# Laying out the probabilities one step later in paged decode attention: a hybrid decoder step on one core

## The chip, the cores and the metric

The kernel runs on one NeuronCore of a Trainium2 chip. The metric is the device time of one execution in microseconds, median of several. The kernel before takes 1250.35 us (three runs, 1250.27 to 1250.57). The profile is of one further execution.

## What is computed

One layer of a hybrid decoder, for a prompt of 512 tokens and for 8 sample sequences of 4 new tokens each, with shared float32 weights: a gated FFN, a mixer (four heads of a gated linear recurrence and four heads of latent attention), and a second gated FFN. The part that matters here is the attention of the sample tokens over 4096 cached rows per sequence, which are fetched through a page table:

```python
past_c = cache_kv_latent[l][page_table].reshape(Bs, past_len, KV_LORA)
past_r = cache_k_rope[l][page_table].reshape(Bs, past_len, QK_ROPE)
...
s = (jnp.einsum('bqhr,bsr->bhqs', ql, c_kv) + jnp.einsum('bqhd,bsd->bhqs', qr, k_rope)).astype(jnp.float32) * scale
s = jnp.where(k_pos[None, None, None, :] <= qp[None, None, :, None], s, -jnp.inf)
p = jax.nn.softmax(s, axis=-1).astype(c_kv.dtype)
return jnp.einsum('bhqs,bsr->bqhr', p, c_kv)
```

## The kernel before

Most of the time is weight matrices. A weight tile (`wraw`, 128x8x128 float32) is loaded by SyncE's DMA queue, split by ScalarE into a rounded high part `wh` (L250) and by VectorE into the rest `wl` (L251), and multiplied with activations that are split in the same way, three matmuls for each product (L259, L277, L288).

The second FFN runs twice: once for the first 256 prompt tokens and once for the others. **Decode runs beside the first of these passes.** `decode()` and the FFN `gb` are two Python generators that the program advances in turn (100 FFN steps over 94 steps of decode). The sample attention is cut into 16 **halves**, two for each sequence: half n is sequence n//2, 2048 cached rows in two gathered blocks. They are called half 0 to half 15 below. Every half goes through a pipeline of five steps `st` = 0 to 4 for each value of n:

- `gather` and `gather_r` (L1366, L1373): GpSimd issues the indirect DMAs for the latent rows (`craw`, seven places: `ulb uhb ha hb mb q0 dx`) and rotary rows (`rraw`, two places).
- `turn(st)` (L1381): VectorE transposes the keys in blocks of 32x32, two instructions for each of five turns, into `kh` (four buffers). Turn 0 takes the rotary rows, turns 1 to 4 take latent columns.
- `score` (L1393): TensorE multiplies. Turns 0 to 2 are used at step 2 (96 row-column groups of matmuls), turns 3 and 4 at step 4 (64). The last of them ends the score, and ScalarE and VectorE copy it to SBUF (L1399); VectorE takes its row maximum (L1401).
- `peak` (L1405 to L1417), at step 1 of the next n: TensorE spreads the maximum (`pm`), VectorE reduces it and makes the bias, ScalarE takes the exponential in place (L1411), VectorE transposes the probabilities into `pt` (L1413), and sixteen small copies place `pt` into `pbuf`, the stationary operand of the value product: four on VectorE, twelve on ScalarE (L1417). `pbuf` and `pt` have two buffers each.
- `value` (L1426), at step 4: TensorE multiplies `pbuf` with the gathered rows, 32 matmuls, 16 for each block. Each run of four matmuls waits for the `pbuf` copies of its own quarter, so for three more of ScalarE's twelve.

In one n, `at(2)` is the half whose scores are computed and `at(3)` the half in front of it, whose peak and value are computed. So at step 4 TensorE has, in this order and with nothing between them, the matmuls of turns 3 and 4 of half k+1 and the value matmuls of half k. Turn 3 is made at step 1 and turn 4 at step 2.

The order of instructions on each engine is not that of the Python code alone: a list scheduler with priorities may move an instruction past others on the same engine. The engines then take their instructions strictly in the order of the compiled program.

The lines touched are those of `peak` (it ends after L1411 and its rest becomes a new function) and the loop of `decode` (`if st == PEAK and at(3)`, with PEAK = 1).

Of the kernel before, what the change touches and what calls it, by code (L numbers as in the profile page):

```python
# [66 lines left out]
PEAK = 1  # L67
# [43 lines left out]
def hybrid_step_kernel(  # L111
# [18 lines left out]
    def mk(shape, dt, tag, bufs=1, pool=None):  # L130
        return (pool or cur[-1]).tile(shape, dt, name=tag, tag=tag, bufs=bufs)
# [10 lines left out]
    def ps(name, tag="ps", own=False):  # L142
        if tag == "ps" and not own:
            tag = CYC[turns[0] % 4]
            turns[0] += 1
        return pp.tile([P, 512], F32, name=name, tag=tag, bufs=NPS[tag])
# [422 lines left out]
    with scope("ffn0") as pool:  # L569
# [143 lines left out]
        if True:  # L713
            if True:
                sst.close()
                st = stg.enter_context(tc.tile_pool(name="st", bufs=1, side="right", reuse_waits="tile"))
# [585 lines left out]
    with scope("dec"):  # L1302
# [49 lines left out]
        class Half:  # L1352
# [50 lines left out]
            def peak(self):  # L1403
                pm = ps("pm", "pm")[:, :P]
                nc.tensor.matmul(pm, self.mx.broadcast_to([P, P]), ident, start=True, stop=True, skip_group_check=True)  # L1405
                m = m3[:, self.i, self.bs]
                nc.vector.tensor_reduce(m, pm.rearrange("p (g q) -> p q g", q=16), axis=AX.X, op=ALU.max)
                mq = mk([P, 16], F32, "mq", 2)
                mb = mk([P, 1], F32, "mbd", 2)
                nc.vector.scalar_tensor_tensor(mq, m, -SCALE, selL, op0=ALU.mult, op1=ALU.mult, accum_out=mb)  # L1410
                nc.scalar.activation(self.e, self.e, AF.Exp, scale=SCALE, bias=mb, accum_out=Lc[:, self.i, 0, self.b : self.b + 1])  # L1411
                pt = mk([P, ROWS, 32], F32, "pt", 2)
                nc.vector.transpose(pt.rearrange("p a k -> p (a k)"), self.e)  # L1413
                for c in range(4):
                    for g in range(4):
                        src = pt[c * 32 : c * 32 + 32, g // 2 * 4 : g // 2 * 4 + 4, g % 2 * 16 : g % 2 * 16 + 16]
                        (nc.scalar.copy if g else nc.vector.tensor_copy)(self.p[g * 32 : g * 32 + 32, c // 2, c % 2 * 4 : c % 2 * 4 + 4, self.i * 16 : self.i * 16 + 16], src)  # L1417
# [19 lines left out]
        def decode():  # L1437
            H = [Half(n) for n in range(NH2)]
            blocks = [h_ for h_ in H for _ in range(2)]
            ups = [(h_, st) for h_ in H for st in range(len(JS))]  # L1440

            def gather(n=1):
                for h_ in blocks[:n]:
                    h_.gather()
                del blocks[:n]

            def turn(top):
                if ups:
                    h_, st = ups.pop(0)
                    with tc.issue_after(top.ins) if top is not None else nullcontext():  # L1450
                        h_.turn(st)
                    if st == 0 and h_.n + 1 < NH2:
                        H[h_.n + 1].gather_r()

            for n in range(NH2 + 4):

                def at(k):
                    return H[n - k] if 0 <= n - k < NH2 else None

                for st in range(len(JS)):  # L1460
                    if at(2):
                        for k in RUNS.get(st, ()):
                            at(2).score(k)
                    if n < 3 and st == 0:
                        if n == 0:
                            H[0].gather_r()
                        gather(2 + n // 2)
                    if st == PEAK and at(3):
                        at(3).peak()
                    if st == 1 and at(4) and at(4).i:  # L1470
                        at(4).gathered()
                    if st == len(JS) - 1 and at(3):
                        for c in range(2):
                            at(3).value(at(4), c)
                            gather()
                    if n > 1 or n == 1 and st >= 1:
                        if n != 2 or st >= 2:
                            turn(at(2).top if at(2) and st == len(JS) - 1 else None)
                    yield

        def decode_end():
# [33 lines left out]
            nc.vector.tensor_copy(oT[1][:, NH:, HS[1] - TS :], o[:, :P].rearrange("p (h t) -> p h t", h=NH))  # L1515

        ga, gn = decode(), decode_new()
        na, ib = len(JS) * (NH2 + 2) + 4, 0
        for ia in range(na):
# [190 lines left out]
```

## Time and profile before

| | |
|---|---|
| median of the runs | 1250.35 us |
| profiled execution, whole | 1243.16 us |
| its span in the trace | 1241.4 us |
| mean granted TensorE clock | 0.999 |
| decode beside the FFN, in the trace | about 711 to 955 us |
| the 16 `pt` transposes (L1413), one for each half | start at 734.9 to 946.9 us, 436 ns each in the median |

The profile's times are those of one execution. "Busy" of an engine is the time in which one of its instructions runs; TensorE's weight loads (PEld) have a row of their own and run ahead of its matmuls. A bracket such as `[0.85 <-DVE pt L1413]` behind an instruction says how long its engine had been idle before it, and what ended that wait. Rows with a count (x12) merge like instructions that follow each other. In the traces the buffers of the pools are called by short names: `q` stands for several small tiles.

### The profile page before, as it was taken

The numbers are of one execution on the slowest core, as the hardware profiler recorded it, in microseconds if no ns is written. First come the engines' busy times: TensorE is split into PE (matmuls) and PEld (weight loads), VectorE is DVE, ScalarE is ACT, GpSimd is POOL, SyncE is SP. The second block draws the span as 40 slices with busy tenths as digits, with TensorE's granted clock in tenths as the row PEclk, the third lists the DMA queues.
The fourth block names the chain that finished last, engine by engine and source line by source line (L and its number), as shares of the span: only waits on it lengthen the run. The fifth ranks groups of instructions, "written<-read, shape, count | busy, mean of one in ns | idle before, by whom it ended". The sixth has DMA issues, their size and how long they took to land.

```text
span 1241.4 us, 29997 instructions
## 1 busy us (share of the span) xinstructions
PE 1215.0 (98%) x12366; PEld 1151.3 (93%) x12366; DVE 982.7 (79%) x1976; ACT 738.8 (60%) x1559; POOL 76.5 (6%) x80
## 2 busy tenths in 40 slices
PE   8999999999999999999999999999999999999997
PEld 6999999999999989988898888888888999999997
DVE  7897788878678888786877899999998778566665
ACT  7675545455366744545758766666656776554455
POOL 0000000000000000000001312322310000000000
PEclk9999999999999999999999999999999999999999
DMA  6232333232264213333233868878776635545451
GB/s 238 86 115 90 103 103 102 86 99 91 62 221 147 82 54 105 88 94 130 85 105 117 339 214 303 310 282 323 258 275 232 198 106 188 184 137 188 150 151 60
DMA packets 73113, 195.59 MB, mean 158 GB/s; under 512 B 12336, under 2 KB 27728, under 8 KB 68240
## 3 DMA queue, kind: packets, MB, share of 16 engines
q1 hardware_dynamic: 64512, 150.47, 37.3%
q0 software_dynamic: 7168, 41.95, 9.2%
q8 instruction: 97, 1.59, 0.5%
q10 hardware_dynamic: 1296, 1.26, 0.3%
q14 instruction: 40, 0.33, 0.1%
HBM read 183.97 MB, written 9.67 MB: 156 GB/s over the span
## 4 chain that ended last, share of the span: by engine, by line
PE 79%; DVE 11%; ACT 7%; issue 2%; DMA 2%; SPq 0%; DVEq 0%; ACTq 0%
PE acc L259 29%; PE acc L277 13%; PE dn L259 8%; PE Y L575 7%; PE X L575 4%; PE Z L575 4%; DVE kh L1381 3%; PE acc L731 3%; DVE wl L251 2%; ACT wh L250 1%; PE s L1393 1%; ACT pbuf L1417 1%; DMA wraw<-w_g 1%; PE pa L952 1%; PE o L1426 1%
## 5 line engine op out<-in xcount | busy, mean ns | idle before, releaser
L250 ACT CAST wh<-wraw 128x1024 fp32r<-128x1024 f32 (+2 forms) x194 | 185.0, 957 | 164.3 <-PE acc L259 103.7
L251 DVE TENSOR_TENSOR wl<-wraw,wh 128x1024 fp32r<-128x1024 f32 (+2 forms) x194 | 214.6, 1108 | 72.2 <-ACT wh L250 71.6
L277 PE MATMUL acc<-uha,wh 128*128 128x256 f32 (+1 forms) x528 | 155.5, 295 | 0.1
L277 PE MATMUL acc<-uha,wl 128*128 128x256 f32 (+1 forms) x528 | 150.0, 285 | 0.8 <-DVE wl L251 0.7
L277 PE MATMUL acc<-ula,wh 128*128 128x256 f32 (+1 forms) x528 | 150.5, 286 | 0.0
L259 PE MATMUL acc<-uhb,wh 128*128 128x288 f32 (+1 forms) x432 | 128.0, 296 | 0.0
L259 PE MATMUL acc<-uhb,wl 128*128 128x288 f32 (+1 forms) x432 | 127.0, 295 | 1.0 <-DVE wl L251 0.8
L259 PE MATMUL acc<-ulb,wh 128*128 128x288 f32 (+1 forms) x432 | 127.5, 295 | 0.0
L277 PEld LDWEIGHTS acc<-uha,wh 128*128 128x128 f32 x528 | 99.2, 188 | 8.8 <-issue 7.9
L277 PEld LDWEIGHTS acc<-uha,wl 128*128 128x128 f32 x528 | 99.2, 188 | 2.3 <-DVE wl L251 1.6
L277 PEld LDWEIGHTS acc<-ula,wh 128*128 128x128 f32 x528 | 99.4, 188 | 1.6 <-issue 1.2
L259 PEld LDWEIGHTS acc<-uhb,wl 128*128 128x128 f32 x432 | 81.2, 188 | 1.6 <-DVE wl L251 1.6
L259 PEld LDWEIGHTS acc<-uhb,wh 128*128 128x128 f32 x432 | 81.0, 187 | 0.2 <-ACT uhb L170 0.2
L259 PEld LDWEIGHTS acc<-ulb,wh 128*128 128x128 f32 x432 | 81.1, 188 | 0.1
L259 PE MATMUL dn<-hh,dh 128*128 128x272 f32 x256 | 74.3, 290 | 0.0
L259 PE MATMUL dn<-hh,dl 128*128 128x272 f32 x256 | 73.7, 288 | 0.0
L259 PE MATMUL dn<-hl,dh 128*128 128x272 f32 x256 | 73.6, 288 | 0.0
L277 PE MATMUL acc<-uhb,wh 128*128 128x272 f32 x176 | 52.8, 300 | 0.0
L1417 ACT COPY pbuf<-pt 32x64 f32<-32x64 f32 x192 | 46.5, 242 | 10.1 <-DVE pt L1413 7.3
L259 PE MATMUL acc<-hlb,wh 128*128 128x288 f32 x176 | 52.1, 298 | 0.0
L259 PE MATMUL acc<-hhb,wh 128*128 128x288 f32 x176 | 51.8, 298 | 0.0
L1393 PE MATMUL s<-kh,q 64*32 64x128 f32 x2560 | 48.0, 273 | 3.5 <-DVE kh L1381 3.5
(632 smaller groups left out, 3881.3 us busy)
## 6 DMA issues: line engine op xcount, KB each, us to landing
wraw<-w_u SPq DMA_DIRECT2D x66, 512.0 KB, 4.3
wraw<-w_g SPq DMA_DIRECT2D x65, 512.0 KB, 3.9
wraw<-w_d SPq DMA_DIRECT2D x40, 384.0 KB, 3.5
wraw<-w_in SPq DMA_DIRECT2D x24, 512.0 KB, 3.5
wraw<-w_d SPq DMA_DIRECT2D x32, 320.0 KB, 3.1
wraw<-w_d SPq DMA_DIRECT2D x16, 512.0 KB, 3.8
wraw<-w_o SPq DMA_DIRECT2D x16, 512.0 KB, 3.7
g_S<-state SPq DMA_DIRECT2D x4, 512.0 KB, 4.4
```

The lines of the kernel that those rows point to most:

```text
L250: nc.scalar.copy(wh[:, :kt], w[:, :kt])
L251: nc.vector.tensor_tensor(wl[:, :kt], w[:, :kt], f32(wh[:, :kt]), op=ALU.subtract)
L259: nc.tensor.matmul(out, a, b, start=n == 0, stop=n == last)
L277: nc.tensor.matmul(acc[:, :n], a[:, k], b[:, k], start=k + i == 0, stop=k == kt - 1 and i == 2)
L575: nc.tensor.matmul(bank, a[p][:, k], b[q][:, k], start=first and k + n == 0, stop=k == 3 and n == 2, skip_group_check=True)
L731: nc.tensor.matmul(accs[x, d], wts[d][p][:, k], hs[k // 2][q][:, k % 2, x], start=k + n == 0, stop=k == nf - 1 and n == 2)
L952: nc.tensor.matmul(po[es, c].rearrange("p (n m) -> p n m", m=m), kx[:, cs], up(qx[:, cs], m), start=True, stop=True, skip_group_check=True)
L1381: nc.vector.transpose(kh[:, g].rearrange("p a j k -> p a (j k)"), src)
L1393: nc.tensor.matmul(self.s[r][c * 32 : c * 32 + 32, :P], q[rs, j], kh, start=st + jj == 0, stop=st == len(JS) - 1 and jj == 1, skip_group_c ...
L1417: (nc.scalar.copy if g else nc.vector.tensor_copy)(self.p[g * 32 : g * 32 + 32, c // 2, c % 2 * 4 : c % 2 * 4 + 4, self.i * 16 : self.i * ...
L1426: nc.tensor.matmul(o[g : g + 32, :R], self.p[:, c, a], self.craw[c][:, a], start=i + c == 0 and a < 4, stop=i + c == 2 and a >= 4, skip_gr ...
```

## The change

`peak` stops after the exponential. Its rest, the transposition of the probabilities and the sixteen copies, becomes `lay`, which is called at the end of step 2 (PEAK + 1), behind that step's turn, which is turn 4.

```diff
                 nc.scalar.activation(self.e, self.e, AF.Exp, scale=SCALE, bias=mb, accum_out=Lc[:, self.i, 0, self.b : self.b + 1])
+
+            def lay(self):
                 pt = mk([P, ROWS, 32], F32, "pt", 2)
                 nc.vector.transpose(pt.rearrange("p a k -> p (a k)"), self.e)
...
                         if n != 2 or st >= 2:
                             turn(at(2).top if at(2) and st == len(JS) - 1 else None)
+                    if st == PEAK + 1 and at(3):
+                        at(3).lay()
                     yield
```

No instruction is added or taken away. TensorE's order is the same row for row, and so are those of SyncE's and GpSimd's queues. ScalarE's order differs in three halves: in half 0 two parts of a sigmoid come between the twelve copies, and in halves 2 and 3 one copy of an FFN result (L390) comes ahead of them instead of behind. VectorE's order is the same in halves 2, 3, 9, 12 and 15 and differs in the others. Three places follow.

VectorE in half 4 (`hb` and `mb` are the two blocks of half 5, so `kh<-hb` and `kh<-mb` are turn 4; `kh<-rraw` is turn 0 of half 6). Before:

```order
L251 TENSOR_TENSOR wl<-wraw,wh 128x1024
L1413 STREAM_TRANSPOSE pt<-q_8192 128x256
L171 TENSOR_TENSOR hla<-sil,hha 128x256
L1417 COPY pbuf<-pt 32x4x16 x4
L1381 STREAM_TRANSPOSE kh<-hb 128x512
L1381 STREAM_TRANSPOSE kh<-mb 128x512
L1381 STREAM_TRANSPOSE kh<-rraw 128x512 x2
L334 TENSOR_TENSOR sil<-acc,rna 128x256
```

And now:

```order
L251 TENSOR_TENSOR wl<-wraw,wh 128x1024
L171 TENSOR_TENSOR hla<-sil,hha 128x256
L1381 STREAM_TRANSPOSE kh<-hb 128x512
L1381 STREAM_TRANSPOSE kh<-mb 128x512
L1415 STREAM_TRANSPOSE pt<-q_8192 128x256
L1381 STREAM_TRANSPOSE kh<-rraw 128x512
L1419 COPY pbuf<-pt 32x4x16 x4
L1381 STREAM_TRANSPOSE kh<-rraw 128x512
L334 TENSOR_TENSOR sil<-acc,rna 128x256
```

Both transposes of turn 4 and one FFN row have moved ahead of `pt`, and one rotary transpose ahead of the copies. Halves 1, 7 and 10 change in the same way, and half 13 does but for one transpose of turn 4 that stood ahead of `pt` already. In halves 0, 5 and 11 `pt` keeps its place in front of turn 4, and only copies move behind the second transpose of it; in half 8 one copy moves behind both.

VectorE in half 6 (`ulb` and `uhb` are the blocks of half 7). Before:

```order
L1413 STREAM_TRANSPOSE pt<-q_8192 128x256
L1381 STREAM_TRANSPOSE kh<-ulb 128x512
L1417 COPY pbuf<-pt 32x4x16 x4
L1381 STREAM_TRANSPOSE kh<-uhb 128x512
L336 TENSOR_TENSOR sil<-sil,sit 128x256
```

And now:

```order
L1381 STREAM_TRANSPOSE kh<-ulb 128x512
L1381 STREAM_TRANSPOSE kh<-uhb 128x512
L1415 STREAM_TRANSPOSE pt<-q_8192 128x256
L336 TENSOR_TENSOR sil<-sil,sit 128x256
L1419 COPY pbuf<-pt 32x4x16 x4
```

Here `pt` moves behind two transposes, and the copies behind an FFN row as well.

VectorE in half 14 (`ha` and `hb` are the blocks of half 15). Before:

```order
L1413 STREAM_TRANSPOSE pt<-q_8192 128x256
L392 TENSOR_TENSOR ma<-ma,acc 128x256
L1417 COPY pbuf<-pt 32x4x16 x4
L1381 STREAM_TRANSPOSE kh<-ha 128x512
L1381 STREAM_TRANSPOSE kh<-hb 128x512
L251 TENSOR_TENSOR wl<-wraw,wh 128x1024
```

And now:

```order
L392 TENSOR_TENSOR ma<-ma,acc 128x256
L1415 STREAM_TRANSPOSE pt<-q_8192 128x256
L251 TENSOR_TENSOR wl<-wraw,wh 128x1024
L1381 STREAM_TRANSPOSE kh<-ha 128x512
L1381 STREAM_TRANSPOSE kh<-hb 128x512
L1419 COPY pbuf<-pt 32x4x16 x4
```

Here a weight split that stood behind turn 4 has moved ahead of it.

## The prediction

> **What bounds the kernel now.** I read the page first, then the busy time by stretches, the waits, and the instructions around single halves.
>
> ```profile
> span 1241.4 us, 29997 instructions
> PE 1215.0 (98%) x12366; PEld 1151.3 (93%) x12366; DVE 982.7 (79%) x1976; ACT 738.8 (60%) x1559; POOL 76.5 (6%) x80
> ```
>
> TensorE is busy for 98% of the span, so a change that leaves its work alone can win only its gaps. The change moves instructions of decode only, so the stretches of decode count. Their columns are start and end, length, then busy us of PE, PEld, DVE, ACT and POOL, the clock, and the DMA share:
>
> ```profile
> 755.00:797.00 42.00, 42.00 (x747) 37.97 (x740) 38.02 (x80) 26.46 (x70) 12.42 (x12) 1.00 0.92 329
> 797.00:840.00 43.00, 41.44 (x855) 35.34 (x858) 40.87 (x93) 28.31 (x82) 12.87 (x13) 1.00 0.77 269
> 881.00:940.00 59.00, 58.56 (x1152) 51.12 (x1154) 55.49 (x128) 36.53 (x106) 11.91 (x11) 1.00 0.71 244
> ```
>
> From 755 to 797 TensorE never stops and VectorE has 4 us to spare. From 797 to 840 (the values of halves 4 to 7) VectorE is busy 40.87 of 43 us and TensorE has gaps: two engines bind there, nearly equally. The stretch from 881 is built in the same way. The chain of waits for 796 to 842 says who carries it:
>
> ```profile
> by line: DVE kh L1381 24.2%; ACT pbuf L1417 11.7%; DVE wl L251 10.8%; issue 6.9%; ACT wh L250 6.4%; PE o L1426 4.1%; PE s L1393 3.9%; PE acc L277 3.6%; ACT sit L321 3.4%; DVE hla L171 2.9%; DVE sil L336 2.8%; ACT sit L322 2.8%; DVE sil L365
> ```
>
> So there it runs through VectorE, and through ScalarE's `pbuf` copies where VectorE has to wait for ScalarE. Now the waits in 715 to 950 us (who waits for whom: us in total, times, longest):
>
> ```profile
> PE s L1393 <- DVE kh L1381: 3.5, 7, 1.4
> DVE wl L251 <- ACT wh L250: 7.4, 15, 0.9
> DVE pt L1413 <- ACT q L1411: 0.4, 1, 0.4
> ```
>
> Two readings. VectorE's `pt` waits for the exponential in one half only, 0.4 us (half 12, whose order stays): there is no stall on the exponential to take away. What can be won is the first row, TensorE waiting for turn 4, 3.5 us in halves 1, 5, 7, 11 and 14.
>
> **The change, half by half.** Half 4, the plain case:
>
> ```profile
> 795.15 0.44 DVE L1413 STREAM_TRANSPOSE pt<-q 128x256 f32<-128x256 f32 x1
> 795.82 0.77 DVE L1417 COPY pbuf<-pt 32x64 f32<-32x64 f32 x4
> 796.61 0.71 DVE L1381 STREAM_TRANSPOSE kh<-hb 128x512 f32<-128x512 f32 x1
> 797.25 0.67 DVE L1381 STREAM_TRANSPOSE kh<-mb 128x512 f32<-128x512 f32 x1
> 797.84 1.26 DVE L1381 STREAM_TRANSPOSE kh<-rraw 128x512 f32<-128x512 f32 x2
> 799.80 1.23 DVE L251 TENSOR_TENSOR wl<-wraw,wh 128x1024 fp32r<-128x1024 f32 x1 [0.38 <-ACT wh L250]
> 795.62 3.07 ACT L1417 COPY pbuf<-pt 32x64 f32<-32x64 f32 x12 [0.85 <-DVE pt L1413]
> 798.72 1.05 ACT L250 CAST wh<-wraw 128x1024 fp32r<-128x1024 f32 x1
> 803.48 1.06 ACT L250 CAST wh<-wraw 128x1024 fp32r<-128x1024 f32 x1 [1.55 <-PE acc L277]
> 798.59 0.59 PEld L1426 LDWEIGHTS o<-uhb,pbuf 128*32 128x32 f32 x16 [0.20 <-issue]
> 800.45 0.19 PEld L277 LDWEIGHTS acc<-uha,wh 128*128 128x128 f32 x1 [0.41 <-issue]
> ```
>
> Starts follow each other by about 0.35 us for the FFN row and 0.6 us for a key transpose, so behind `hla` and two key transposes `pt` ends 1.53 us later, at 797.12. VectorE itself loses nothing by that, the same rows stand there. But **ScalarE's twelve copies wait for `pt`, and they are the long piece: 3.07 us.** They move from 795.62 to 797.15 and end at 800.22 instead of 798.69. Turn 4 is ready 1.2 us earlier, which nobody needs here. What value does then can be seen in half 15, where the copies are late already:
>
> ```profile
> 947.82 3.07 ACT L1417 COPY pbuf<-pt 32x64 f32<-32x64 f32 x12
> 950.17 0.16 PEld L1426 LDWEIGHTS o<-hb,pbuf 128*32 128x32 f32 x8 [0.60 <-ACT pbuf L1417]
> 950.94 0.16 PEld L1426 LDWEIGHTS o<-hb,pbuf 128*32 128x32 f32 x8 [0.61 <-ACT pbuf L1417]
> 951.51 0.30 PEld L1494 LDWEIGHTS pb<-q,ones 128*128 128x128 f32 x2 [0.41 <-issue]
> ```
>
> The groups of four matmuls start 0.77 us apart, at the pace of three copies; the last starts 0.05 us after the last copy (950.89), and TensorE's next work 0.57 us after that. So TensorE goes on no earlier than **last copy + 0.62 us**. In half 4 that is 800.84 instead of 800.45: **+0.39 us**.
>
> Behind the copies in ScalarE's queue stands `wh` (798.72), and VectorE's `wl` waits for it: 801.33 instead of 799.80. From there VectorE is 1.53 us late, and up to half 7 it never waits for TensorE in a way that would give this back; ScalarE does, once (1.55 us for a buffer at 803.48), but VectorE stands behind its own order. That last row also says that the weights are as far ahead as their buffers allow, so a late `wl`, and the late weight DMA that SyncE's queue issues when `wraw` comes free, reach no matmul. GpSimd's gathers are queued behind the rotary transposes and the value, which move by these same 1 to 3 us. The waits hold no row in which a transpose waits for a gather, so I take them at nothing; if their room is less than that, their lateness is that of half 7 in rival 4.
>
> Half 5 (`pt` stays, copies behind turn 4) and the two after it:
>
> ```profile
> 808.84 3.07 ACT L1417 COPY pbuf<-pt 32x64 f32<-32x64 f32 x12 [1.16 <-DVE pt L1413]
> 810.84 0.37 PEld L1393 LDWEIGHTS s<-kh,q 64*32 64x32 f32 x24 [0.55 <-DVE kh L1381]
> 813.27 0.19 PEld L277 LDWEIGHTS acc<-uha,wh 128*128 128x128 f32 x1 [0.41 <-issue]
> 822.82 0.42 ACT L322 ACTIVATE sit<-sit 128x256 f32<-128x256 f32 x1
> 823.27 3.07 ACT L1417 COPY pbuf<-pt 32x64 f32<-32x64 f32 x12
> 827.53 0.19 PEld L277 LDWEIGHTS acc<-uha,wh 128*128 128x128 f32 x1 [0.41 <-issue]
> 836.79 3.06 ACT L1417 COPY pbuf<-pt 32x64 f32<-32x64 f32 x12 [0.66 <-DVE pt L1413]
> 841.57 0.19 PEld L288 LDWEIGHTS acc<-hha,wh 128*128 128x128 f32 x1 [0.41 <-issue]
> ```
>
> Half 5: turn 4 gains the 0.74 us of the copies and inherits 1.53, so the wait at 810.84 comes 0.8 later instead of going away. The copies end at 811.91 + 1.53 = 813.44, TensorE goes on at 814.06: +0.79 in all.
>
> Half 6: `pt` starts 1.53 late and behind two transposes, and ends at 825.82. Before, the copies began when the sigmoid ended (823.24), now with `pt`: at 825.85, to 828.92, TensorE at 829.54: **+2.01**. The `wh` behind them makes VectorE 2.57 us late.
>
> Half 7: `pt` ends at 836.76 + 2.57 + 1.52 = 840.85, the copies at 843.95, TensorE at 844.57 instead of 841.57: **+3.00**. The 1.38 us that it waited for turn 4 are gone, and it stands before the copies. Behind it (840 to 881) TensorE alone binds, ScalarE waits for its buffers again, and VectorE falls back into step. So halves 4 to 7 cost 3.0 us.
>
> Half 1 has the order of half 4, ahead of the stretch where only TensorE binds, so its lateness ends there:
>
> ```profile
> 750.98 3.07 ACT L1417 COPY pbuf<-pt 32x64 f32<-32x64 f32 x12 [0.66 <-DVE pt L1413]
> 752.74 0.15 PEld L1393 LDWEIGHTS s<-kh,q 64*32 64x32 f32 x8 [1.65 <-DVE kh L1381]
> 755.76 0.19 PEld L288 LDWEIGHTS acc<-hha,wh 128*128 128x128 f32 x1 [0.41 <-issue]
> ```
>
> Turn 4 comes 1.2 us earlier, but the copies end at 754.05 + 1.46 = 755.51 and TensorE goes on at 756.13: +0.37. Halves 2 and 3: ScalarE's copies 0.38 us later by one FFN copy, with over 3 us until their value: nothing. Half 0: value comes a whole microsecond after the copies, nothing. Half 8: `pt` as before, nothing.
>
> Halves 10 to 15 repeat 4 to 9 in their first part; then come
>
> ```profile
> 922.90 3.07 ACT L1417 COPY pbuf<-pt 32x64 f32<-32x64 f32 x12 [1.38 <-DVE pt L1413]
> 926.85 0.19 PEld L259 LDWEIGHTS acc<-hha,wh 128*128 128x128 f32 x1 [0.41 <-issue]
> 941.45 0.19 PEld L277 LDWEIGHTS acc<-uha,wh 128*128 128x128 f32 x1 [0.41 <-issue]
> ```
>
> Halves 10 and 11 give +0.8 as 4 and 5 do; 12 keeps its order and adds nothing; in half 13 `pt` is behind one more transpose (0.66) and 1.53 late, copies to 928.16, TensorE 928.78: +1.9. In half 14 a weight split (1.18 us) comes ahead of turn 4, against copies of 0.76 that go behind it: turn 4 is 0.45 + 2.1 us late, +2.6. In half 15 TensorE waited for copies anyway (1.2 us in the two rows above), and ScalarE is less late than TensorE: about 0.5 comes back. Sum +2.1.
>
> **Sum:** 0.37 + 3.0 + 2.1 = 5.5 us. After 955 us TensorE alone binds, so that it stays. Against the profiled execution: span 1241.4 to 1246.9, execution 1243.16 to 1248.7. The median of the runs lies 7.2 us above that execution; I add the same to it: **1250.35 + 5.5 = 1255.8 us.**
>
> The cost that the trace doesn't show is how far lateness is handed on. If each half stood alone, VectorE in step at its start, the same rows give: +0.37 +0.39 −0.4 +0.5 +0.4 in halves 1, 4, 5, 6, 7 and +0.39 −0.4 +0.35 +0.45 in 10, 11, 13, 14, so +2.0. If nothing were given back after half 7 (ScalarE 4.1 us late there) and in half 15, it would be some 8.5. I take 5.5, by the chain of waits, which shows no step of TensorE between 798.7 and 838.
>
> **The rivals.** (1) *Faster:* TensorE's wait for turn 4 goes and none takes its place: −3.5 us, or −4.5 with the restarts of its pipe behind them, so 1246. It decides if ScalarE's copies end before the score does. For it speaks the wait row; against it, that in half 1 the copies ended at 754.05, already after the value's start at 753.90 in the trace. The Trainium skill (Perfetto Trace Analysis, Optimization Strategy) would give this one: look at the gaps of the engine that should be saturated, find the instruction that it waits for, and let that one start sooner. The trace's row names the transposes of turn 4, and the change does let them start sooner; by that rule alone the time would be this rival's. Chance 0.12. (2) *Each half alone*, lateness swallowed by ScalarE's idle time (it is busy 28.31 of 43 us): 1252.4. Chance 0.2. (3) *Nothing*, since five halves keep their order and TensorE's order is unchanged: 1250.4. Against it: ten halves do change. Chance 0.1. (4) *More*, lateness handed on past half 7: 1259 and above. Chance 0.08.
>
> **How the numbers follow.** The forecast has 0.5. The range leaves out (1) and (4), 0.2 together: 1249 to 1259; both ends of the unknown cost lie in it. A measurement of this kernel can tell about 0.2%, 2.5 us, from no change. Slower by more: the forecast, (4) and a little of (2), 0.61. Within: the rest of (2) and (3), 0.27. Faster: (1), 0.12.
>
> **What would show it.** In the changed profile: TensorE's wait for `kh` goes in halves 1 and 7 and stays in 5 and 11; a wait of its weight loads for ACT `pbuf`, in steps of 0.77 us, stands in halves 1, 4, 6, 7, 10 and 13; VectorE's wait for `wh` grows from 7.4 us by 4 or more; ScalarE's copies start 1.5 us later against the score in halves 1, 4, 7, 10. The prediction is wrong if the copies turn out not to be what value waits for, or if VectorE is back in step before half 6.

## The result and the profile after

The changed kernel takes **1259.08 us** (median of 6 runs, 1258.27 to 1261.13), the kernel before beside it 1250.31 us (6 runs, 1249.65 to 1251.63). The ratio is 1.0071, with a 95% interval of 1.0061 to 1.0081: 8.8 us slower. The forecast was slower by 5.5 us, 1255.8, with a range up to 1259.0. The sign and the side are right, the size is not.

One thing must be known before the profiles can be compared. The kernel before was timed in seven sessions (runs taken together on one chip), and it has two levels: about 1244 us in four of them (1243.8, 1244.0, 1244.7, 1244.1) and about 1250 us in three (1250.3, 1250.9, 1250.6). One chip showed both. The profile of before that the prediction is made from (1243.16 us) is of the lower level; the times that it was added to, and the profile of after below (1259.4 us whole), are of the upper one. Whether that profile of before comes from the same chip as the three times beside it is not on record.

Of the profile after, first the page's span and busy times, then the same three stretches, then the waits in 715 to 950 us:

```profile
span 1257.6 us, 30020 instructions
PE 1227.6 (98%) x12366; PEld 1156.5 (92%) x12366; DVE 983.7 (78%) x1976; ACT 739.9 (59%) x1559; POOL 72.9 (6%) x80
```

```profile
755.00:797.00 42.00, 40.93 (x660) 34.65 (x650) 33.99 (x68) 24.91 (x66) 11.99 (x12) 0.96 0.83 286
797.00:840.00 43.00, 41.24 (x771) 33.82 (x771) 37.92 (x87) 26.18 (x73) 11.38 (x12) 1.00 0.74 250
881.00:940.00 59.00, 56.52 (x1048) 47.02 (x1048) 51.44 (x117) 32.37 (x91) 14.47 (x15) 1.00 0.73 255
```

```profile
PEld s L1393 <- issue: 14.3, 28, 0.6
DVE wl L251 <- ACT wh L250: 13.5, 14, 1.8
PE s L1393 <- issue: 7.0, 23, 0.3
PEld o L1428 <- issue: 4.8, 19, 0.6
```

The row that the change went for, TensorE waiting for turn 4 (`PE s L1393 <- DVE kh`, 3.5 us), is gone. VectorE's wait for `wh` grew from 7.4 to 13.5, as forecast. But the row that was to grow, TensorE waiting for ScalarE's `pbuf`, is missing. In its place TensorE stops inside the score, for 14.3 us at weight loads and 7.0 at matmuls, and the profile finds nothing that it waits for ("issue"). The two rows are for the most part the same pauses, seen at the loads and again at the matmuls behind them: with the overlap counted once they are 14.8 us. (Some of the expectations below use the sum, 21.3.) The kernel before had no such row in its profile at the lower level. Half 4 shows what that looks like, in the weight loads and in ScalarE's copies (start, length, row):

```profile
803.09 0.64 PEld L1393 LDWEIGHTS s<-kh,q 64*32 64x32 f32 x45
804.12 0.16 PEld L1393 LDWEIGHTS s<-kh,q 64*32 64x32 f32 x3 [0.40 <-issue]
804.86 0.19 PEld L1393 LDWEIGHTS s<-kh,q 64*32 64x32 f32 x5 [0.57 <-issue]
...
806.73 0.59 PEld L1428 LDWEIGHTS o<-uhb,pbuf 128*32 128x32 f32 x16 [0.20 <-issue]
802.74 3.06 ACT L1419 COPY pbuf<-pt 32x64 f32<-32x64 f32 x12 [2.38 <-DVE pt L1415]
```

The first 45 matmuls of the run go at full pace, the last 19 or so come in small groups 0.75 us apart. The copies are over at 805.80; value starts at 806.73 and waits for nobody. So here TensorE is late by itself, and the copies' lateness is hidden behind it. Is that the change's doing, or the level's? The experiments begin there.

### The profile page after: what moved, and what is told of

It reads as the page before. It is cut to its first block, busy times and chain, and to the rows that moved or that the text cites. A ratio compares the mean times of both kernels' runs of the same rounds, so it can differ in the third digit from the quotient of the medians.

```text
span 1257.6 us, 30020 instructions
## 1 busy us (share of the span) xinstructions
PE 1227.6 (98%) x12366; PEld 1156.5 (92%) x12366; DVE 983.7 (78%) x1976; ACT 739.9 (59%) x1559; POOL 72.9 (6%) x80
## 3 DMA queue, kind: packets, MB, share of 16 engines
q8 instruction: 97, 1.59, 0.5%
## 4 chain that ended last, share of the span: by engine, by line
PE 89%; DVE 4%; ACT 4%; issue 1%; DMA 1%; DVEq 0%; SPq 0%; ACTq 0%
PE acc L259 30%; PE acc L277 18%; PE dn L259 8%; PE Y L575 6%; PE X L575 4%; PE Z L575 4%; PE s L1393 4%; PE acc L731 3%; PE o L1428 2%; PE pa L952 1%; PE acc L288 1%; ACT wh L250 1%; PE s L1202 1%; DMA wraw<-w_g 1%; DVE wl L251 1%
## 5 line engine op out<-in xcount | busy, mean ns | idle before, releaser
L251 DVE TENSOR_TENSOR wl<-wraw,wh 128x1024 fp32r<-128x1024 f32 (+2 forms) x194 | 214.6, 1108 | 80.2 <-ACT wh L250 78.5
L1393 PE MATMUL s<-kh,q 64*32 64x128 f32 x2560 | 55.9, 273 | 7.4 <-issue 7.0
L1393 PEld LDWEIGHTS s<-kh,q 64*32 64x32 f32 x2560 | 39.0, 105 | 19.7 <-issue 14.3
```

Of the source, the lines that this page charges most:

```text
L251: nc.vector.tensor_tensor(wl[:, :kt], w[:, :kt], f32(wh[:, :kt]), op=ALU.subtract)
L1393: nc.tensor.matmul(self.s[r][c * 32 : c * 32 + 32, :P], q[rs, j], kh, start=st + jj == 0, stop=st == len(JS) - 1 and jj == 1, skip_group_c ...
```

## The experiments

Theory A is the prediction's: late `pt`, late copies on ScalarE, lateness handed on through the weight split. Theory B came from the profile after: since VectorE's copies now stand behind turn 4, value waits for two engines, and the semaphore instructions in PE's sequencer at value's line rise from 36 to 59; they might slow the issue. Theory C: the slow issue belongs to a session's level.

### Both kernels again

Before, unchanged, and after, unchanged:

> The kernel before, profiled once more, nothing changed. Theory C (TensorE's slow issue belongs to single executions, not to the change): a second profile shows it too, its idle time on the score's line L1393 put down to issue rises from about 1 us to 5 or more and its span from 1241.4 to about 1248. Theories A (late ScalarE copies) and B (a second semaphore on the value matmuls): the span stays within 2 us of 1241.4, and 36 semaphore instructions of 51 ns stand at value's line.

> The changed kernel, profiled once more, nothing changed. Theory C: its idle time on the score's line put down to issue (21.3 us on PE and PEld together in the first profile) differs by 5 us or more between the two profiles, and the halves that show the slow issue are not the same ones. Theory B: the same halves (0, 1, 4, 6, 7, 9, 10, 12) show it again, span within 2 us of 1257.6.

Measured, in one session: before 1243.74, one time (15 runs of it beside: 1243.82, 1242.74 to 1245.78), after **1249.48**, one time. The change now costs 5.7 us. The waits of this second profile of after (715 to 960 us):

```profile
DVE wl L251 <- ACT wh L250: 16.4, 15, 2.9
PEld o L1428 <- ACT pbuf L1419: 12.7, 27, 0.7
PEld s L1393 <- DVE kh L1381: 5.0, 8, 1.6
PE s L1393 <- issue: 1.4, 1, 1.4
```

Here is the profile that the prediction described: the wait for ScalarE's `pbuf` is the largest of TensorE, and the slow issue is gone but for one pause of 1.4 us. The chain of waits for 796 to 846 us, of the same profile, gives the copies 21.5% where it was 11.7%:

```profile
by line: DVE kh L1381 28.3%; ACT pbuf L1419 21.5%; DVE wl L251 10.4%; issue 7.7%; ACT wh L250 5.9%; DVE hla L171 3.7%; DVE pt L1415 2.8%; DVE sil L336 2.5%; DVE sil L365 2.1%; ACT sit L321 2.1%; PE acc L288 1.8%; ACT sit L322 1.7%; DVE mxh 
```

And half 6, which was to add most, has four groups of value in the step of three copies (0.77 us), and TensorE goes on at 830.07, 0.63 us behind the last copy (826.38 + 3.06):

```profile
827.18 0.16 PEld L1428 LDWEIGHTS o<-q,pbuf 128*32 128x32 f32 x8 [0.34 <-ACT pbuf L1419]
827.96 0.16 PEld L1428 LDWEIGHTS o<-q,pbuf 128*32 128x32 f32 x8 [0.62 <-ACT pbuf L1419]
...
829.50 0.16 PEld L1428 LDWEIGHTS o<-dx,pbuf 128*32 128x32 f32 x8 [0.61 <-ACT pbuf L1419]
826.38 3.06 ACT L1419 COPY pbuf<-pt 32x64 f32<-32x64 f32 x12 [1.05 <-DVE pt L1415]
```

For the kernel before, what came is what theories A and B had said: no row of issue in the score, a span of 1241.9 us, 36 semaphore instructions. For the changed kernel it is what theory C had said: the slow issue went from one profile to the next. And it went although the 59 semaphore instructions stayed, which speaks against theory B.

### Two engines to wait for

Only VectorE's four copies (g = 0) move behind turn 4; `pt` and ScalarE's copies (`place(range(1, 4))`) stay in `peak`:

```diff
-                    for g in range(4):
+                    for g in gs:
...
+                self.place(range(1, 4))
...
+                    if st == PEAK + 1 and at(3):
+                        at(3).place((0,))
```

> The kernel before with one thing of the change: VectorE's four copies into pbuf go behind the two transposes of the score's last part; pt, its twelve ScalarE copies and TensorE's order stay. The transposes come up to 0.74 us sooner, the score's wait no longer implies those copies, and value waits for two engines. Theory A: nothing is late, so 1247 to 1251. Theory B: the slow issue of the changed kernel is there in the same halves, 59 or so semaphore instructions at value's line, 1255 to 1262.

Measured: 1241.98 us (11 runs) against 1243.82, ratio 0.9988 (0.9979 to 0.9997). It has 57 semaphore instructions at value's line and no slow issue (one pause of 0.7 us), and it is a little faster than before. At this level the changed kernel had no slow issue either, so this alone doesn't decide on theory B; a run at the upper level does. e8_half15 below, of the same order up to half 15, has 57 of these instructions there and 4.0 us of issue at the score's weight loads, where the kernel before has 36 and 6.6. Theory B falls. The row that the change went for shrinks without anything being late:

```profile
PEld s L1393 <- DVE kh L1381: 3.0, 5, 1.0
PEld o L1430 <- ACT pbuf L1421: 2.1, 6, 0.6
PE s L1393 <- DVE kh L1381: 0.9, 2, 0.8
```

### More and less on ScalarE

The changed kernel with all sixteen copies on ScalarE (e1_act_only, the first line with +), and with eight and eight (e3_after_8_8, the second):

```diff
-                        (nc.scalar.copy if g else nc.vector.tensor_copy)(self.p[...
+                        nc.scalar.copy(self.p[...
+                        (nc.scalar.copy if g > 1 else nc.vector.tensor_copy)(self.p[...
```

> The changed kernel with all sixteen copies into pbuf on ScalarE, so that value waits for one engine where it waited for two. ScalarE's block of copies grows from 3.07 to about 4.1 us. Theory A (the copies bind): 1.0 us later in each half whose copies bind, 1 to 8 us slower than the changed kernel: 1260 to 1267. Theory B (the wait for VectorE beside that for ScalarE slows TensorE's issue): the slow issue in the score goes, 36 or fewer semaphore instructions at value's line, and the time falls to 1247 to 1254 although the copies are later.

Measured: 1258.80 us (4 runs), 15 us above before in that session and 9.3 above the one time of the changed kernel beside it, a little more than theory A's 1 to 8. Its waits:

```profile
DVE wl L251 <- ACT wh L250: 34.9, 16, 3.7
PEld o L1428 <- ACT pbuf L1419: 22.5, 30, 1.0
```

1.03 us more on ScalarE in each half nearly doubled the wait for `pbuf` and doubled VectorE's wait for `wh`.

> The changed kernel with eight of the sixteen copies into pbuf on VectorE and eight on ScalarE, where it was four and twelve. ScalarE's block falls from 3.07 to about 2.05 us, VectorE's grows from 0.74 to about 1.5 us. Theory A (the ScalarE block behind the late pt binds, and its lateness is handed on through the weight split behind it): the opposite of the kernel with all sixteen on ScalarE; TensorE's wait for ScalarE's pbuf falls from 12.7 us to under 5 and most of the 5.7 us over the kernel before comes back: 0 to 2.5 us above it. Rival (VectorE's queue is what is late): 0.75 us more work on VectorE in each half makes it slower than the changed kernel, 6 to 12 us above the kernel before.

The changed kernel itself ran in that session too:

> The changed kernel once more, timed. If the 8.8 us of the first timing belong to the change alone, it stands 7.5 to 10 us above the kernel before whatever that one's level is. If the first timing was made where TensorE's slow issue adds to both kernels (1250.3 for the kernel before, against 1243.8 in the second call), then at a level of 1244 for before the changed kernel stands 5 to 6.5 us above it, its profile shows less than 3 us of idle time put down to issue on the score's line and some 12 us of waits for ScalarE's pbuf; at a level of 1250 it stands 8 to 10 above, with 15 us or more of issue.

Measured: eight and eight 1249.42 us (6 runs) against 1243.97, ratio 1.0035 (1.0023 to 1.0048); the changed kernel 1250.26 (5 runs), ratio 1.0046 (1.0033 to 1.0059), 6.3 us above before as its second case said, with 1.2 us of issue in the score. Under eight and eight the wait for `pbuf` halves, from 13.0 to 6.2 us, but only 0.8 us comes back, less than the two intervals can tell apart. VectorE took the work over, and in its narrow stretch it has no room:

```profile
797.00:840.00 43.00, 42.55 (x830) 36.83 (x816) 41.44 (x102) 24.01 (x63) 12.89 (x12) 1.00 0.74 258
```

41.44 us busy of 43. Neither expectation held: 5.5 us above before lies between the 0 to 2.5 of the one and the 6 to 12 of the other. My reading is that ScalarE's block binds and VectorE's queue has nothing to spare. The same move on the order of e2_dve_late shows the second of these alone:

> The kernel of e2_dve_late (pt and ScalarE's copies at the peak, VectorE's copies behind the last two transposes) with eight copies on each engine. Theory A: the copies bound only in half 15, where TensorE waited 1.5 us for them; there about 1 us comes back: 0.5 to 1.5 us under e2_dve_late, 2 to 3.5 us under the kernel before. Rival (VectorE's queue): 0.75 us more on VectorE delays the transposes of the halves behind, 1 to 6 us above e2_dve_late.

Measured: 1246.26 us (11 runs), ratio 1.0016 (1.0007 to 1.0024), some 4 us above e2_dve_late. The rival held. Half 15's wait for `pbuf` did go (1.5 us to 0).

### Half 4 alone, and the halves without 4 to 7 and 10 to 14

The late order only where it is asked for; here for half 4 (e5_half4). In e7_rest the same two lines ask for `self.n in (4, 5, 6, 7, 10, 11, 13, 14)` and for the halves not in that list:

```diff
+                if self.n != 4:
+                    self.lay()
...
-                    if st == PEAK + 1 and at(3):
+                    if st == PEAK + 1 and at(3) and at(3).n == 4:
```

> The kernel before with the change in half 4 alone: there pt and its sixteen copies go behind the two transposes, everywhere else they stay at the peak. Theory A with lateness handed on (the forecast): TensorE's first weight load behind the value is 0.4 us later in half 4, and the 1.5 us by which VectorE's weight half is late show up as 1.0 to 1.5 us in half 5, which keeps the order of before, and stay up to half 7. Rival (each half alone): +0.4 us in half 4, and no more than that in halves 5 to 7.

Measured: 1246.39 us, one time, 2.4 above before (1243.97, 17 runs). Half 4's end, the weight split on VectorE behind it and half 5's score:

```profile
801.03 0.16 PEld L1430 LDWEIGHTS o<-ha,pbuf 128*32 128x32 f32 x8 [0.30 <-ACT pbuf L1421]
801.60 0.19 PEld L277 LDWEIGHTS acc<-uha,wh 128*128 128x128 f32 x1 [0.41 <-issue]
802.09 1.23 DVE L251 TENSOR_TENSOR wl<-wraw,wh 128x1024 fp32r<-128x1024 f32 x1 [1.85 <-ACT wh L250]
...
811.74 0.15 PEld L1393 LDWEIGHTS s<-kh,q 64*32 64x32 f32 x8 [0.35 <-DVE kh L1381]
813.12 0.37 PEld L1393 LDWEIGHTS s<-kh,q 64*32 64x32 f32 x24 [1.23 <-DVE kh L1381]
...
815.55 0.19 PEld L277 LDWEIGHTS acc<-uha,wh 128*128 128x128 f32 x1 [0.41 <-issue]
```

Decode starts later in this execution than in the before of the other session, so only steps from half to half count. Against that profile (787.90, 800.55, 813.36 at the ends of halves 3, 4 and 5), and with 788.58 at the end of half 3 here, half 4 adds 0.37 us and half 5 another 1.14: its wait for turn 4 was 0.53 and is 1.58. The row of `wl` shows the step between: it waits 1.85 us for `wh`, in that profile 0.38, and starts 1.52 us later against the end of half 3. Halves 6 to 15 add nothing and give nothing back. **The lateness is handed on**; the rival, each half alone, falls.

> The changed kernel with halves 4, 5, 6, 7, 10, 11, 13 and 14 put back as before: the late pt and copies only in halves 0 to 3, 8, 9, 12 and 15. Theory A (the loss is made in the two chains 4 to 7 and 10 to 14): by the forecast's terms +0.4 us in half 1 and nothing elsewhere, so 0 to 1 us above the kernel before on the same chip. Rival (each half costs its share): half of the halves, half of the 6 us: +3.

Measured: 1251.49 us, with the kernel before at 1250.87 (12 runs), the upper level: +0.6, one time. Half by half, against e9_before of the same session, it is +0.7 in half 0, +0.7 in half 1 and +0.2 in halves 2 to 14 together; decode starts 0.45 us sooner. The loss is made in the two chains, and in half 0, where the forecast had nothing, and half 1.

### The two levels

> The kernel before once more, for its level on this chip. At a level of 1250 its profile shows 5 us or more of idle time put down to issue on the score's line, which the profiles at 1243 lack, and the changed kernel's extra 3 us (8.8 in the first timing against 6 here) are of that kind; at a level of 1244 it has none and that stays open.

The kernel before stood at the upper level here. The waits in this third profile of before (1250.13 us; 715 to 960 us):

```profile
PEld s L1393 <- issue: 6.6, 12, 0.6
PE s L1393 <- issue: 3.3, 11, 0.4
PEld s L1393 <- DVE kh L1381: 2.8, 4, 1.3
PE s L1393 <- DVE kh L1381: 1.7, 4, 1.0
```

So before has the slow issue too at 1250, 6.7 us of it with the overlap of the two rows counted once, and the whole difference of its levels lies in decode: from the start of half 0's last 64 score matmuls to TensorE's first work behind half 15 it takes 219.4 us (739.02 to 958.46), at 1244 it took 213.1 (738.58 to 951.67). That is 6.3 us, and the two times differ by 6.4. Halves 4 to 7 have no part in it: they take 53.8 us at both levels. Then the changed kernel, in two sessions:

> The changed kernel once more. If the level decides: at 1244 for the kernel before it stands 5 to 7 us above it, with 10 us or more of waits for ScalarE's pbuf and under 3 us of idle time put down to issue on the score's line; at 1250 it stands 8 to 10 us above, with some 20 us of such idle time, 1.5 us or more of it in each of halves 4, 7 and 10, and no waits for pbuf ahead of half 15. If the 8.8 us belonged to the first session alone, it stands 5 to 7 above at 1250 too.

> The changed kernel, another session, the same two cases as for e11_after, which met a level of 1244: at 1250 for the kernel before, 8 to 10 us above it with some 20 us of idle time put down to issue on the score's line if the level decides, 5 to 7 us if the first session's 8.8 was its own.

The first met the lower level: 1250.61 (4 runs) against 1244.08, ratio 1.0050 (1.0033 to 1.0067). The second met the upper one: **1259.96 (4 runs) against 1250.59, ratio 1.0073** (1.0057 to 1.0090). The change costs about 6 us at the one level and 9 at the other, and the first result is of the second kind. The intervals of single sessions still overlap; what tells the two apart is that two sessions stand on either side, and the profiles. Its waits at the upper level are those of the first profile, 15.2 us counted once:

```profile
PEld s L1393 <- issue: 14.4, 27, 0.6
PE s L1393 <- issue: 7.5, 22, 0.6
```

Last, half 4 alone, in the same two sessions:

> The kernel of e5_half4 once more (the change in half 4 alone). At a level of 1250, if the late pt is what brings the slow issue into half 4: 1.5 to 2.5 us of idle time put down to issue in that half's score, and none in halves 6, 7 and 10, where the changed kernel has it; if not, none in half 4 either. At a level of 1244 it repeats e5_half4: 0.4 us in half 4, 1.1 in half 5, kept to the end.

> The change in half 4 alone, the same two cases as for e12_half4: at a level of 1250, 1.5 to 2.5 us of idle time put down to issue in half 4's score if the late pt brings it there, none if not; at 1244 the 0.4 and 1.1 us of e5_half4.

At 1244 it repeats e5_half4 (1247.05 us; half 4 adds 0.37, half 5 1.15). At 1250 it takes 1258.15 us, 7.6 above before. Single times hold what lies ahead of decode too, so here is the same stretch as above, in us:

| from half 0's score to the end of half 15 | at 1244 | at 1250 |
|---|---|---|
| before (e0_before, e9_before) | 213.1 | 219.4 |
| half 4 alone (e5_half4, e14_half4) | 214.6 | 225.4 |
| after (e0_after, e13_after) | 219.8 | 230.1 |

These are one execution each. One late half costs 1.5 us at the lower level and 6.0 at the upper one; all of them 6.7 and 10.7. In halves 4 to 7 at the upper level one late half costs as much (5.8) as the whole change (5.3 and 5.9 in its two profiles there). Half 4 of e14_half4, where before has no slow issue at either level:

```profile
802.51 0.65 PEld L1393 LDWEIGHTS s<-kh,q 64*32 64x32 f32 x46
803.60 0.14 PEld L1393 LDWEIGHTS s<-kh,q 64*32 64x32 f32 x3 [0.43 <-issue]
...
805.85 0.19 PEld L1393 LDWEIGHTS s<-kh,q 64*32 64x32 f32 x8 [0.59 <-issue]
```

The late order of one half brings 2.2 us of slow issue into that half. This holds in every profile at this level: the run takes 3.6 to 3.7 us in the three with half 4 late (after, e13_after, e14_half4) and 1.09 in the three with it early (e9_before, e7_rest, e8_half15). Halves 5, 6 and 7 of e14_half4, whose order is that of before, get it as well, in score or value (1.4, 1.8 and 2.1 us); half 10 does not. So my expectation was right for half 4 and wrong for halves 6 and 7: it isn't the half's own order that does it. What these halves share can be worked out from rows: the lead, from the end of turn 4 on VectorE to the start of the last 64 score matmuls (the 64th weight load ahead of value), and the length of that run, which is 1.09 us where nothing stops it. At 1250, in us, from e9_before, e13_after and e8_half15 (of which more below; its `pt` is early and VectorE's four copies are late):

```
half                0    1    2    3    4    5    6    7    8    9   10   11   12   13   14
before   lead     1.2 -0.7  2.6  2.4 -0.4 -1.1 -0.4 -2.2  2.6  2.2 -0.4 -1.1  0.3  2.4  1.0
         run      2.9  1.6  1.7  1.2  1.1  1.7  1.1  2.9  1.8  2.4  1.1  1.7  3.8  1.1  1.1
after    lead     1.9  0.6  2.6  2.4  0.7  0.7  2.3  1.1  3.5  1.8  0.7  0.7  2.1  2.7  0.0
         run      3.7  4.0  1.7  1.2  3.7  1.1  3.3  3.3  1.2  2.8  3.7  1.1  2.2  1.1  1.1
e8       lead     2.0  0.2  2.6  2.4  0.4 -0.2  0.0 -1.6  2.1  2.2  0.4 -0.3 -0.3 -0.3 -1.1
         run      3.0  1.7  1.7  1.2  1.1  1.1  1.1  2.2  2.5  2.4  1.1  1.1  1.1  1.1  1.7
```

In halves 2 to 14, where turn 4 ends behind the start of the run, the run is longer by its wait for turn 4, if it has one, and shows no slow issue. Where turn 4 ends ahead, the run may be slow. Half 1 is an exception: in e9_before turn 4 ends 0.7 us behind the start, and the run has a pause of 0.6 us put down to issue all the same. The change turns the lead round in halves 1, 4 to 7, 10 and 11. In halves 4, 6, 7 and 10 the run is then slow where it was not; in 5 and 11 it goes at full pace, and the value behind it is slow in its stead (some 1.4 us each). In these halves the lead is needed, but it is not enough: halves 3, 13 and 14 have it and go at full pace or nearly, and at the level of 1244 the same lead of 0.7 in half 4 gives a run of 1.4. Half 12 shows the turn the other way: with a lead of 0.3 to 0.4 its run takes 3.7 to 3.8 us (e9_before, e7_rest, e14_half4), and in e8_half15, where turn 4 ends 0.3 us behind the start, 1.1.

### A version that is faster than both

e2_dve_late with eight and eight copies in half 15 alone:

```diff
-                self.place(range(1, 4))
+                self.place(range(2 if self.n == 15 else 1, 4))
...
-                        at(3).place((0,))
+                        at(3).place((0, 1) if at(3).n == 15 else (0,))
```

> The kernel of e2_dve_late with eight copies on each engine in half 15 alone, where TensorE waited 1.5 us for ScalarE's copies. Theory A: ScalarE's block ends 1.0 us sooner there and nothing else moves: 0.7 to 1.3 us under e2_dve_late, 2.3 to 3.3 us under the kernel before. Rival (VectorE's queue costs as much as in e4_before_8_8, where all halves lost 4.3 us, 0.27 each): 0.3 us above e2_dve_late.

> The kernel of e8_half15 once more. At a level of 1244 for the kernel before: 2.3 to 3.3 us under it, as the sum of e2_dve_late's 1.8 and 1.0 in half 15 says. If the 3.6 us at the level of 1250 came from less of TensorE's slow issue alone, it stands at 1244 within 1 us of the kernel before. At a level of 1250: 3 to 4 under it again.

Measured, at 1250: 1247.25 (8 runs) against 1250.87, ratio 0.9975 (0.9964 to 0.9986). At 1244: **1240.80 (9 runs) against 1244.66, ratio 0.9973** (0.9963 to 0.9983). That is 3.6 and 3.9 us, at the lower level more than the 2.3 to 3.3 of theory A, but with an interval (2.1 to 4.6 us) that holds them, and not a matter of the slow issue alone. In half 15 value and the step to the next work take 1.86 us (947.42 to 949.28), in e2_dve_late 2.54 (947.32 to 949.86): 0.7 us, a little under the 1.0 expected, since value's own pace binds once the copies are in time. The rest of the gain in decode is that of e2_dve_late: from half 0's score to the end of half 15 it takes 210.7 us in e10_half15, 211.4 in e2_dve_late and 213.1 in e0_before. That nothing else moves was not so: behind half 15 the compiled order of TensorE differs in 39 rows (at 952 to 979 us in the kernel before), and from there to the end it takes 289.5 us, where e2_dve_late takes 290.6 and e0_before 290.3. Part of the 3.9 us is of that. The two kernels with eight and eight copies and the one with all sixteen on ScalarE differ there too, and take 288.7 to 289.5 us.

## Why the prediction was right in its steps and wrong in its sum

Its steps can be held against the second profile of after, which is of the level that it was worked out at. These are TensorE's first weight loads behind value in halves 1, 4, 5, 6, 7, 13, 14 and 15:

```profile
756.27 0.19 PEld L288 LDWEIGHTS acc<-hha,wh 128*128 128x128 f32 x1 [0.41 <-issue]
801.40 0.19 PEld L277 LDWEIGHTS acc<-uha,wh 128*128 128x128 f32 x1 [0.41 <-issue]
814.62 0.19 PEld L277 LDWEIGHTS acc<-uha,wh 128*128 128x128 f32 x1 [0.41 <-issue]
830.07 0.19 PEld L277 LDWEIGHTS acc<-uha,wh 128*128 128x128 f32 x1 [0.41 <-issue]
845.10 0.19 PEld L288 LDWEIGHTS acc<-hha,wh 128*128 128x128 f32 x1 [0.41 <-issue]
932.53 0.19 PEld L259 LDWEIGHTS acc<-hha,wh 128*128 128x128 f32 x1 [0.41 <-issue]
947.72 0.19 PEld L277 LDWEIGHTS acc<-uha,wh 128*128 128x128 f32 x1 [0.41 <-issue]
957.80 0.30 PEld L1498 LDWEIGHTS pb<-q,ones 128*128 128x128 f32 x2 [0.41 <-issue]
```

Each less its row of before, which the prediction shows; half 3 ended at 787.80 before and at 788.38 here, half 9 at 873.50 and 877.33 (decode starts 0.45 us sooner in this execution: its 64 matmuls of half 0's score at 738.04, before at 738.49). The last column is the same at the level of 1250, where the median was measured: the first profile of after and e13_after, each less e9_before (whose first row holds some 0.8 us of a stretch at half clock, of which the last section tells):

| step | forecast | measured at 1244 | at 1250 |
|---|---|---|---|
| half 0 and half 1 | +0.37 | +0.96 (0.51 + 0.45) | +2.9, +3.0 |
| halves 4 to 7, end of 7 against end of 3 | +3.0 | +2.95 | +5.3, +5.9 |
| of it half 4, half 5, half 6, half 7 | 0.39, 0.40, 1.22, 0.99 | 0.37, 0.40, 1.19, 0.99 | |
| halves 8 and 9 | 0 | +0.3 | -0.2, -0.1 |
| halves 10 to 13, against the end of 9 | +1.9 | +1.85 | +1.6, +1.9 |
| halves 10 to 14 | +2.6 | +2.44 | |
| halves 10 to 15 | +2.1 | +2.46 | +1.6, +2.0 |
| span | +5.5 | +6.3 | |

**Right, at the level of 1244:** the rule "last copy + 0.62 us", the late ScalarE block as what value waits for, the handing on through `wh` and `wl` (half 4 alone showed it by itself), the size in both chains within 0.2 us up to half 14, and that half 5 keeps its wait for turn 4. It repeats: e6_after and e11_after, of the same level, have halves 4 to 7 and 10 to 15 within 0.03 us of e0_after's 56.72 and 80.47. **Off by a little:** halves 0 and 1 (0.6 more), halves 8 and 9 (0.3 more) and half 15, where the half microsecond did not come back. They make the 6.3 (with the 0.45 us of the earlier start, 6.7) out of 5.5. Of the first, 0.2 us lies in half 0, whose copies were to have a whole microsecond to spare.

**Wrong in a sign that cost nothing:** TensorE's wait for turn 4 was to go in halves 1 and 7. At the lower level 1.6 and 1.2 us of it stay (2.1 and 1.8 before, by the weight loads): in half 1 it was longer than the 1.2 us that turn 4 gained, and in half 7 turn 4 inherits VectorE's lateness. The copies end behind it in both, so the sum didn't feel it. At 1250 that wait did go, and slow issue stands in its place. The wait for `pbuf` in steps stands, at the lower level, in halves 1, 6, 7 and 13; in halves 4 and 10 it is one wait of 0.3 us.

**The rivals.** *Faster* fell, and e2_dve_late shows under which condition its sign would have held: the Trainium skill (Perfetto Trace Analysis, Optimization Strategy) says to let the instruction that the gapped engine waits for start sooner; done with nothing else made late, that took TensorE's wait for turn 4 from 3.6 to 0.9 us and gained 1.8 us. The measurement decides for the rule there, and against it in the changed kernel, where the same start was bought with `pt`. *Each half alone* fell with e5_half4. *Nothing* fell with the result. *More* gave the right number for a wrong reason, which is luck: the lateness was not handed on past half 7 (halves 8 and 9 add 0.3 us at the lower level and none at the upper).

**The step that failed** is the one behind the sum: "The median of the runs lies 7.2 us above that execution; I add the same to it". I took 7.2 us as something that stands beside the change. It was not. As far as e9_before shows it for its session, it is TensorE's slow issue inside decode's scores, 6.7 us of idle time at 1250, in the very matmuls whose timing the change moves, and the change makes it 15. At that level TensorE's lateness takes the form of slow issue instead of waits for copies, and half 4 alone costs 6.0 us of decode where it costs 1.5 at the lower level. So the same change is worth +6.3 and +6.5 (timed, sessions at 1244) and +8.8 and +9.4 (at 1250). The prediction had named this as a sign of being wrong: "if the copies turn out not to be what value waits for". At 1250 they are not, ahead of half 15. Of the 3.3 us that the result lies above 5.5, about 0.8 is the size of the small terms above, and the rest is this step.

What stays open: why a session has the one level or the other, and what TensorE stands still for in those 0.6 us gaps. The lead in the table above is a condition found by comparing halves, and half 12 of e8_half15 is its only test in the other direction, in one execution and a kernel made for something else. One candidate for the gaps that was not tested is the delivery of TensorE's instructions. The DMA view of e9_before lists a queue `q8 instruction: 97, 1.59, 0.5%`, and 1.59 MB would be 64 bytes for each of TensorE's 24,732 weight loads and matmuls, if it is theirs. One of its packets starts at 915.08 us, beside the slow run of half 12 at 915.11, but another starts at 799.96, just ahead of half 4's run, which goes at full pace. That settles nothing.

## To carry to other kernels

When the profiled execution is some microseconds off the median of the runs, find out where those microseconds lie before adding them to a sum: if they lie in the stage that is changed, they are a term of the sum and not an offset. Before moving a producer behind other work of its engine, look at the longest block that hangs on it, here ScalarE's 3.07 us of copies: it becomes late with the producer, and its lateness travels through whatever the same queue does next. If only the start of the other work is wanted, move what does not sit on the long block: moving VectorE's four copies alone gained 1.8 us where the whole move lost 6.

## What the runs showed of the hardware that was not expected

**Slow issue of TensorE.** In three of seven sessions, runs of 64 short matmuls (1.09 us at full pace) go on for up to 3.8 us: mostly after 40 to 50 of them, groups of three to ten come some 0.75 us apart, with no wait that the profile shows. In the kernel before it adds 6 to 7 us. In halves 2 to 14 of the six profiles of those sessions every such run had turn 4 over ahead of it; in half 1 two did not.

**A stretch at half clock.** In some executions the granted clock is 0.50 for 3.4 us (in two of them for 10.2) at about 692 to 698 us, ahead of decode. In the changed kernel a second stretch of 3.4 us falls on half 1's value in four of five profiles (the third column from the right is the clock; the second profile of after first, then that of e6_after):

```profile
755.00:759.00 4.00, 3.87 (x39) 2.98 (x40) 2.00 (x5) 3.13 (x9) 2.71 (x3) 1.00 0.68 186
```

```profile
755.00:759.00 4.00, 3.90 (x31) 1.91 (x32) 2.02 (x4) 3.82 (x13) 2.88 (x4) 0.57 0.61 165
```

None of the three profiles of before has it there. From the end of half 0 to the end of half 2 the execution with it takes 32.28 us, the one without 31.45: it costs 0.8 us. Both executions are of the lower level, so it is not what makes the levels. But it is a part of what the change costs where it falls: the one execution without it took 5.7 us more than before, and the two sessions at that level 6.3 and 6.5.
